# Hybrid decoder step on one core: attention's small TensorE work gathered into fewer, larger groups

## The chip, the cores and the metric

The kernel runs on one core of one Trainium2 chip. The metric is the device time in microseconds (us) of one execution; the median of three runs of the kernel before is 1492.1 us (1491.84 to 1492.78).

## What is computed

One layer of a hybrid decoder: a half-step SwiGLU network, then two branches side by side (gated linear attention, GLA, and stick-breaking attention, SB), their gated sum, and a second half-step SwiGLU network. There are 512 prompt tokens, 16 meta tokens ahead of them and 32 sample tokens (8 sequences of 4, each with 256 cached keys): 560 columns in all. The part that the change touches is the stick-breaking attention:

```python
def block(args):                                   # 16 heads of 64
    qblk, qi = args
    z = jnp.einsum('bqhd,bkhd->bhqk', qblk, k) * scale + bias_f
    mask = k_idx[None, :] < qi[:, None]
    l = jnp.where(mask, jax.nn.log_sigmoid(-z), 0.0)
    r = lax.cumsum(l, axis=3, reverse=True) - l
    a = jnp.where(mask, jnp.exp(jax.nn.log_sigmoid(z) + r), 0.0)
    return jnp.einsum('bhqk,bkhd->bqhd', a, v)
```

So a weighting is sigmoid(z) times the product of (1 - sigmoid(z)) over the later keys; the kernel gets that product from a running scan.

## The kernel before

All large products run on TensorE as three products of float32r parts (a rounded part "hi" and the rest "lo"): hi by hi, hi by lo, lo by hi. A weight tile is loaded by a DMA of the SP queue (`raw`), cast to hi on ScalarE (ACT, `S.copy`), and its lo is a subtraction on VectorE (DVE, line 172). Each group of six such matmuls ends with a `yield`, and the loop then calls `step()`. The text counts in these steps: **a step is six main matmuls**. Whatever else is to be done is put in tables of step numbers (`then(n, f)` for attention, `when(n, f)` for the mixer after it, `later(n, f)` relative to now), and a function that comes due at a step issues all its instructions there. Every engine but SP runs its instructions in exactly that program order, so the table of step numbers is the order on each queue.

The stick-breaking stage takes eight pairs of heads (`Pair`, `pr` 0 to 7). The main stream of a pair is 8 steps of query products (`queries`, lines 728 to 731) and 14 steps of key and value products (`values_keys`, `seven_steps`, lines 1079 to 1081: seven half products in place of eight, in the order a by b1, d by b1, b by t, d by b2, c by t, a by b2, c by t4, two steps each; `a`, `d`, `b`, `c` are PSUM banks, `b1`, `t`, `b2`, `t4` weight parts). While the main stream of pair `pr + 1` runs, the attention of pair `pr` is strewn in at steps `n + d`, where `n` is the first step of that stream:

- `scores(e, 0..2)` (e is the head of the pair; lines 2009 and 2010): four or two matmuls into one PSUM bank, then two sigmoids on ACT (`keep`, `beta`, lines 2013 and 2014) and masks on GpSimd (POOL, line 2018).
- `scan(e, 0..3)` (line 2027) on DVE: the running products. `weigh(e)`: one long DVE multiplication (128x1343) that gives the weightings.
- `turned(e, 0..2)` (line 2089): transposes of the weightings on TensorE, each copied out by ACT (line 2092). `meta_turned` does this for the meta tokens (lines 2115, 2116).
- `summed` (line 2105) and `meta_summed` (lines 2120, 2122): the value sums.
- `rows_v`, `rows_k`, `tails` (lines 2055, 2044, 2064 to 2066): transposes that bring values and keys to the outputs' layout.
- in pairs 4 to 7, `sample_keys` (line 2192, copied by ACT at 2194): transposes of cached key pages, and `sample_products` (line 2206): scores against them.
- `sample_rows` and `sample_rows_out` (lines 2157, 2159, 2171): once, masks for the samples.

All these small outputs share four PSUM banks (`ps`), taken in turn. `Arena` hands out SBUF places; which place a tile gets is a table of bytes, `PLACES`, written ahead of time for this order of takes.

The weight parts of the next pair are cast and subtracted in the same steps: b1 at 2 and 3, t at 5 and 6, b2 at 10 and 11, t4 at 13 and 15. The loads of half of these weights add into `raw` by a DMA of POOL (`st.add`, line 674).

Of the kernel before, what the change touches and what calls it, by code (L numbers as in the profile page):

```python
# [50 lines left out]


PLACES = bytes.fromhex("""
0c4236301f4f2a3d163453647c0256726c6088544a94901c187648867866922414128c8e748a5c00847e684106706e7a80620408244c581a5b07
2e826a28265c4e231e0a062a5e5a3e3c30401e082292784e8c66748e1284207e6886008a0c43104c62047a6e1a585c708036253a826a601c1802
549456640c6c4a9033422c852a5272302e76484e2615882f1046297c840c246c892b13363a42723b282a3038324e102e472f6c1452242b88892a
3a122d4e283332720e0c304246526d73242e114e88103b72322c3a422852316c262a254e46241110723230423a526c6d880e31254e2924517210
504442526d893a305144286c4f88722489504e3b51263a5428426c464488728e8c941e867a80744f68606457517866008a705a6e921c3a361a18
55381614123c0c641a1c2a324e3057182451550c641931241c1b565251311a552419271a55192752511c1a1d1b0c5a2a3e64001a3c1b01030400
0205552750201e384636221970788a72644e5084488e0824260a3d88606c7e3052666a3a824b45473779421f86928c901b7a3e43123923738b21  # L60
7180191d181a30577c7407683c32761233941606146e55624031807e584c30886052564a0732336d6c5552666a068c8256923e3286907a5a3010
6c2e0c54720a5e86365c2a2c0e78181a3a32462851444f201904420070718a1e221c388b299110024e54724c490a323a1a462e567a824800664b
9290296a185185420c061e847071588e443005288c6c040854028a725e2c0e2a1c4c103e4e0082931858390c866691516a90707142843849784a
92185a205c22004854362826026c8a8c58042e7237448208390c0a387a568691246a66253a901e1a78648a8e5593421c49584a348c6c82707204
32304c085e8452864e507a91923e562a0d061e37420a581a2f5530240c088c4c4a49100e5642323458372a04450749060c1e420e47442a2c551a
1c588c06560c044c242e4207371e1a49553230443435100e068c3a4238371c3004550c2432492b1e1a55078c1c2c0637100e4230463804443a34
2a4332071e090c248c55491c1a34062b303242492a0b8c0e244d303a04441e1a1c384637422c8c58100c3255062e304649372a422c3034350810
0e0b2a8c061e1a1c380444372e3a2c56240c0849432a0a3a55308c2e0437428c0624351e381a1c462c442a04434b308c49080a322e550d1e2a49
37303442042e1e30340e1009448c2c1a1c324638068c0a553a240c344b49205c571a2c463a4d3443378438087a902a495e26285c8430044b2e32
5456451a0a068c4284381e5e20364d082c5c321c587a905c2a20491a18422e8c4530324b080a4d36062c04907a04308c84385e04061e2e2c5c2a  # L70
20494237341e063008494b2c32465e5c42394d0a20364432044b3b494a2c00023708221e065c5a303244483600043b4a4c372c4302390a06485a
5e44205c1e2242000a1c263b06048d541a3656185884907a8c484c0f0e06104a243a0c8c283837392c0e04900a08020007367a062a34103b3a2f
0c46080a2a2c37062e7b2f0c4e307c827a62923994663e706e8668403c728a166a7678457e1480125c742a5a1a5e6c1c182660427f89841e4c64
75582220568e7489886c2e542c747f45483b0a02248a8926496036427e1982048c72067c892a1a181c7e805e085b5a1589785c768e886a80147e
3f5f86896987683c9412258b7d3a09734616900788830b006212287a92704266906484741e3e7e2280385654264c6c6a36201a2a184a6010944e
0c78028e521a312e500e0a048c061612143a5a7624085e44682b35832c542a728656883d34421c8a437c481830763283405d772c3d543f69575b
8a432a685a7688554230821b5f69342e8b3e198a3d3c761c182a4654595a68578b4288835f8a3c32182a3e1954821a348b444059696876305f2a
888a83823c188b421a5a6859463e5f2a76548a69403c8842828b5989461a5f545a2a402c6876888a6a828e028010060c8c922a94907866707404
427e6c120a7a22524e3a1e40285e5a5c54202e2a1c30783666221e1a3c7018192c2a22207823181f1e21792a2e1e201f78232179222a54123e20
34322242471e78703c335a64443082922062  # L80
""")


# [53 lines left out]
def hybrid_step(  # L137
# [1377 lines left out]
    with tc.manual_schedule(engines={E.PE, E.DVE, E.Activation, E.Pool}):  # L1515
# [278 lines left out]
        for j in range(5):  # L1794
            n = P if j < 4 else NTL
# [387 lines left out]
    def pages_of(src, c, b0):  # L2183
        return {(b, pg): page(src, 2 * b + pg, c) for b in (b0, b0 + 4) for pg in range(2)}
# [304 lines left out]

    z, kT = take(512), {}  # L2490
    E = mybir.EngineType
    SK, SP, TURN = (4, 7, 13, 14), (9, 16), (15, 16, 17, 18, 19, 20)

    TILE, PAIR, MIX0 = 8, 14, 24
    BEGIN = [0, 3 * TILE]
    while len(BEGIN) < 9:
        BEGIN.append(BEGIN[-1] + TILE + PAIR)
    with tc.manual_schedule(engines={E.PE, E.DVE, E.Activation, E.Pool}):
        kps, mixer_at, at = {}, {}, {}

# [100 lines left out]
        n = 0  # L2601
# [29 lines left out]
        n = 8 * len(PAGES)  # L2631
# [43 lines left out]
        n = 0  # L2675
# [126 lines left out]
```

## Time and profile before

| | |
|---|---|
| median of 3 runs | 1492.1 us |
| the profiled execution: its time, its span | 1492.38 us, 1490.7 us |
| TensorE matmuls (PE) busy | 1477.2 us, 99% of the span, 11825 matmuls |
| DVE, ACT, POOL busy | 74%, 55%, 6% |
| granted TensorE clock | 0.999 |
| stick-breaking stage | some 590 to 820 us after the start |

The profile names engines PE (matmuls), PEld (weight loads), DVE, ACT, POOL and SP. A row of the timeline has start, duration, engine, source line, operation, tiles, shape, count, and in brackets the idle time of the engine before it and what ended it. Durations of neighbouring matmuls overlap, since they are pipelined: what a matmul costs TensorE is the distance from its start to the next start.

### The profile page before, as it was taken

What the parts mean: (1) busy time and instruction counts of PE and PEld (TensorE: products, weight loads), DVE (VectorE), ACT (ScalarE), POOL (GpSimd) and SP (SyncE); (2) the same over time, 40 slices, a digit from 0 to 9 for tenths busy, and PEclk for the clock granted to TensorE, in tenths of its full rate; (3) what the DMA queues carried; (4) which work ended last, traced back from release to release, by engine and by line L of the source; (5) the groups of instructions that cost most, each with busy time, mean ns of one, the idle gap of its engine ahead of it and who ended that gap; (6) DMA issues with size and microseconds to landing.
All of it is one profiled execution on the core that took longest, in us unless ns stands there. A gap on an engine that the chain in (4) does not pass through costs nothing.

```text
span 1490.7 us, 29755 instructions
## 1 busy us (share of the span) xinstructions
PE 1477.2 (99%) x11825; PEld 1426.3 (96%) x11825; DVE 1099.8 (74%) x1844; ACT 822.7 (55%) x1537; POOL 86.6 (6%) x175
## 2 busy tenths in 40 slices
PE   9999999999999999999999999999999999999998
PEld 8999999999999899889888999999999999999998
DVE  6888888855677866888887754676567898888544
ACT  7455445533555657777777543644564455455334
POOL 2000000000000111422111000000000000000000
PEclk9999999999999999999999999999999999999999
DMA  8133333224665596557577857434531333333253
GB/s 252 44 99 96 104 88 104 85 79 128 175 141 129 159 201 141 115 109 148 139 112 187 249 136 205 96 104 137 166 109 54 100 100 100 100 105 93 80 168 100
DMA packets 288541, 187.61 MB, mean 126 GB/s; under 512 B 10988, under 2 KB 266674, under 8 KB 288402
## 3 DMA queue, kind: packets, MB, share of 16 engines
q1 hardware_dynamic: 280706, 181.97, 45.8%
q0 software_dynamic: 7680, 3.74, 2.4%
q8 instruction: 93, 1.52, 0.4%
q14 instruction: 46, 0.38, 0.1%
q10 hardware_dynamic: 16, 0.00, 0.0%
HBM read 160.63 MB, written 25.03 MB: 125 GB/s over the span
## 4 chain that ended last, share of the span: by engine, by line
PE 53%; DVE 3%; ACT 1%; DMA 1%; issue 0%; DVEq 0%; SPq 0%; ACTq 0%
PE acc L1300 4%; PE acc L1301 4%; PE acc L1302 4%; PE acc L1079 3%; PE acc L744 3%; PE acc L742 3%; PE acc L741 3%; PE acc L1080 3%; PE acc L1081 3%; PE acc L728 3%; PE acc L731 3%; PE acc L729 3%; PE ps L2105 1%; DVE room L172 1%; PE ps L2089 1%; PE acc L1239 1%
## 5 line engine op out<-in xcount | busy, mean ns | idle before, releaser
L172 DVE TENSOR_TENSOR room<-room,room 128x560 f32<-128x560 f32 (+15 forms) x469 | 303.3, 666 | 82.1 <-ACT room L808 17.8
L172 DVE TENSOR_TENSOR lo<-raw,hi 128x1024 fp32r<-128x1024 f32 (+1 forms) x207 | 248.2, 1200 | 101.3 <-ACT hi L1006 62.4
L1301 PE MATMUL acc<-room,hi 128*128 128x280 f32 (+1 forms) x896 | 259.7, 290 | 0.0
L1300 PE MATMUL acc<-room,hi 128*128 128x280 f32 (+1 forms) x896 | 259.4, 290 | 0.0
L1302 PE MATMUL acc<-room,lo 128*128 128x280 f32 (+1 forms) x896 | 259.0, 289 | 0.0
L1006 ACT CAST hi<-raw 128x1024 fp32r<-128x1024 f32 x114 | 119.5, 1052 | 141.2 <-PE acc L1301 48.4
L728 PE MATMUL acc<-room,hi 128*128 128x280 f32 x608 | 175.7, 306 | 0.3 <-DVE room L175 0.3
L1302 PEld LDWEIGHTS acc<-room,lo 128*128 128x128 f32 x896 | 168.7, 188 | 0.0
L1301 PEld LDWEIGHTS acc<-room,hi 128*128 128x128 f32 x896 | 168.5, 188 | 0.0
L1300 PEld LDWEIGHTS acc<-room,hi 128*128 128x128 f32 x896 | 168.4, 188 | 0.0
L729 PE MATMUL acc<-room,hi 128*128 128x280 f32 x608 | 163.6, 288 | 0.0
L1079 PE MATMUL acc<-room,hi 128*128 128x280 f32 x476 | 146.2, 307 | 0.4 <-ACT acc L1069 0.2
L1081 PE MATMUL acc<-room,lo 128*128 128x280 f32 (+1 forms) x476 | 138.3, 290 | 0.0
L1080 PE MATMUL acc<-room,hi 128*128 128x280 f32 (+1 forms) x476 | 138.1, 290 | 0.0
L706 ACT CAST hi<-raw 128x1024 fp32r<-128x1024 f32 (+1 forms) x93 | 93.6, 1007 | 78.3 <-issue 20.4
L1006 ACT CAST hi<-room 128x1024 fp32r<-128x1024 f32 x106 | 88.7, 836 | 82.1 <-PE acc L1301 58.7
L172 DVE TENSOR_TENSOR lo<-room,hi 128x1024 fp32r<-128x1024 f32 x106 | 101.1, 954 | 43.7 <-ACT hi L1006 43.4
L731 PE MATMUL acc<-room,lo 128*128 128x280 f32 x608 | 125.9, 288 | 0.0
L728 PEld LDWEIGHTS acc<-room,hi 128*128 128x128 f32 x608 | 114.5, 188 | 7.3 <-issue 5.6
L729 PEld LDWEIGHTS acc<-room,hi 128*128 128x128 f32 x608 | 114.8, 189 | 0.6
L741 PE MATMUL acc<-room,hi 128*128 128x280 f32 (+2 forms) x388 | 110.8, 295 | 0.1
L742 PE MATMUL acc<-room,hi 128*128 128x280 f32 (+2 forms) x388 | 108.8, 290 | 0.0
(409 smaller groups left out, 3606.8 us busy)
## 6 DMA issues: line engine op xcount, KB each, us to landing
raw<-in_w_in_dram SPq DMA_DIRECT2D x68, 256.0 KB, 5.0
raw<-in_ffn_w_gate_dram SPq DMA_DIRECT2D x64, 256.0 KB, 3.1
raw<-in_ffn_w_up_dram SPq DMA_DIRECT2D x64, 256.0 KB, 3.4
raw<-in_ffn_w_down_dram SPq DMA_DIRECT2D x36, 448.0 KB, 3.7
raw<-in_w_in_dram SPq DMA_DIRECT2D x29, 512.0 KB, 6.9
out_dram<-room SPq DMA_DIRECT2D x36, 256.0 KB, 3.4
room<-in_cache_k_dram SPq DMA_DIRECT2D x32, 256.0 KB, 6.7
room<-in_cache_v_dram SPq DMA_DIRECT2D x32, 256.0 KB, 6.1
```

The source lines that it names most:

```text
L172: (eng or V).tensor_tensor(out=out, in0=a, in1=b, op=op)
L728: T.matmul(acc[h][:, :w], hi[k], act.get(k, h, w)[0], start=(k == order[0]), stop=False, skip_group_check=True)
L729: T.matmul(acc[h][:, : wid[h]], hi[k], a[h][1], start=False, stop=False, skip_group_check=True)
L731: T.matmul(acc[h][:, : wid[h]], lo[k], a[h][0], start=False, stop=(k == order[-1]), skip_group_check=True)
L741: T.matmul(acc[h][:nw, : wid[h]], wh, a[h][0], start=(k == 0), stop=False)
L1006: S.copy(hi[:, :kt], src)
L1079: T.matmul(x[:, :n], hi, act_[k][0][:, :n], start=(first and k == 0), stop=False, skip_group_check=True)
L1080: T.matmul(x[:, :w], hi, act_[k][1][:, :w], start=False, stop=False, skip_group_check=True)
L1081: T.matmul(x[:, :w], lo, act_[k][0][:, :w], start=False, stop=(k == 3), skip_group_check=True)
L1300: T.matmul(x[:, :QW], hi, act[k][0], start=(first and k == 0), stop=False, skip_group_check=True)
L1301: T.matmul(x[:, :QW], hi, act[k][1], start=False, stop=False, skip_group_check=True)
L1302: T.matmul(x[:, :QW], lo, act[k][0], start=False, stop=(k == 3), skip_group_check=True)
```

## The change

New numbers in the tables of steps. The scores, the transposes and the sums of a pair come due at fewer steps, so that TensorE meets them in fewer, larger groups between main matmuls (steps 3, 6, 11, 16, 19 for pairs 0 to 3, and 14 besides in pairs 4 to 7). DVE's scans and `weigh` keep the last steps that they had (14 and 15), with some earlier ones moved. `sample_keys` in the mixer and `sample_rows_out` move by one step. `PLACES` is written anew for the new order. No instruction is added or taken out.

```diff
-    SK, SP, TURN = (4, 7, 13, 14), (9, 16), (15, 16, 17, 18, 19, 20)
+    SK, SP, TURN = (14, 14, 14, 14), (16, 16), (16, 16, 16, 19, 19, 19)
...
-            now, n, after = Pair(pr), BEGIN[pr + 1], BEGIN[pr + 2] if pr < 7 else BEGIN[8] + 20
+            now, n, after = Pair(pr), BEGIN[pr + 1], BEGIN[pr + 2] if pr < 7 else BEGIN[8] + 18
...
-            pieces = [(2, now.scores, 0, 0), (3, now.scores, 0, 1), (3, now.meta), (4, now.scan, 0, 0), (4, now.scan, 0, 1), (5, now.scores, 0, 2),
-                      (6, now.scan, 0, 2), (7, now.scan, 0, 3), (6, now.rows_v), (7, now.scores, 1, 0), (9, now.scan, 1, 0), (10, now.scan, 1, 1),
-                      (10, now.weigh, 0), (10, now.scores, 1, 1), (12, now.scan, 1, 2), (11, now.rows_k), (12, now.scores, 1, 2), (12, now.tails),
-                      (14, now.scan, 1, 3), (15, now.weigh, 1)]
+            pieces = [(3, now.scores, 0, 0), (3, now.scores, 0, 1), (4, now.meta), (5, now.scan, 0, 0), (5, now.scan, 0, 1),
+                      (6, now.scores, 0, 2), (6, now.scores, 1, 0), (6, now.rows_v), (8, now.scan, 0, 2), (8, now.scan, 0, 3), (9, now.scan, 1, 0),
+                      (10, now.weigh, 0), (11, now.scores, 1, 1), (11, now.scores, 1, 2), (11, now.rows_k), (11, now.tails),
+                      (13, now.scan, 1, 1), (13, now.scan, 1, 2), (14, now.scan, 1, 3), (15, now.weigh, 1)]
             pieces += [(TURN[i], now.turned, i // 3, i % 3) for i in range(6)] + [(TURN[5], now.meta_turned)]
...
-            then(after + 1, now.summed)
-            then(after + 2, now.meta_summed)
+            then(after + 3, now.summed)
+            then(after + 3, now.meta_summed)
...
                 for d, (q, b) in zip(SK, ((q, b) for q in range(2) for b in (pr - 4, pr))):
                     then(n + d, sample_keys, b, q, kps, kT)
                 for q in range(2):
                     then(n + SP[q], sample_products, 0, pr - 4, q, kT, z)
...
-        then(BEGIN[2] + 13, sample_rows_out)
+        then(BEGIN[2] + 14, sample_rows_out)
...
-                for n, k in enumerate((1, 2, 5, 6)):
+                for n, k in enumerate((2, 2, 5, 5)):
                     when(8 * i + k, use_keys, b0, n)
...
 PLACES = bytes.fromhex("""
-0c4236301f4f2a3d163453647c0256726c6088544a94901c187648867866922414128c8e748a5c00847e684106706e7a80620408244c581a5b07
+1e1218555a06420c505e52908e8070488a7a7e667668946a3264868c4c7c6038842a883462283c742672240a544e6e000292042c4a6c78823e2c
```

How this moves instructions is seen at three places. On TensorE, in the stream of a pair, the transposes of the first head's weightings (line 2089, `ps<-ident,room`) stand between main matmuls of `seven_steps`. Before:

```order
L2089 MATMUL ps_6918<-ident,room_72_4268 128x128 x4
L1079 MATMUL acc_6811<-room_121_6658,hi_6840 128x280
L1080 MATMUL acc_6811<-room_122_6659,hi_6840 128x280
L1081 MATMUL acc_6811<-room_121_6658,lo_6841 128x280
L1079 MATMUL acc_6811<-room_124_6689,hi_6840 128x280
L1080 MATMUL acc_6811<-room_83_4730,hi_6840 128x280
L1081 MATMUL acc_6811<-room_124_6689,lo_6841 128x280
L2089 MATMUL ps_6934<-ident,room_72_4268 128x128 x3
```

On TensorE, at the same place of the change:

```order
L1081 MATMUL acc_6809<-room_121_6659,lo_6830 128x280
L2089 MATMUL ps_6925<-ident,room_5_73 128x128 x4
L2089 MATMUL ps_6931<-ident,room_5_73 128x128 x3
L2089 MATMUL ps_6936<-ident,room_5_73 128x128 x3
L1079 MATMUL acc_6811<-room_110_6520,hi_6760 128x280
L1080 MATMUL acc_6811<-room_111_6521,hi_6760 128x280
```

Ten transposes that stood in three groups with a step between them now stand in one; those of the second head likewise, one step later than their first stood before.

On ACT, at the start of a pair's stream, stand the copy of the value sums (line 2122), the sigmoids of the first scores (2013, 2014) and the casts to hi of two weight parts (1006: b1 from `raw`, t from a room). Before:

```order
L2122 COPY room_127_7496<-ps_7720 128x512
L2013 ACTIVATE room_129_7738<-ps_7739,sbb 128x416
L2014 ACTIVATE room_79_4590<-ps_7739,sbb 128x416
L1006 CAST hi_7748<-raw_7431 128x1024
L2013 ACTIVATE room_129_7738<-ps_7757,sbb 128x416
L2014 ACTIVATE room_79_4590<-ps_7757,sbb 128x416
```

On ACT, at the same place of the change:

```order
L1006 CAST hi_7727<-raw_7429 128x1024
L2122 COPY room_76_4272<-ps_7736 128x512
L2013 ACTIVATE room_125_7283<-ps_7747,sbb 128x416
L2014 ACTIVATE room_5_73<-ps_7747,sbb 128x416
L2013 ACTIVATE room_125_7283<-ps_7756,sbb 128x416
L2014 ACTIVATE room_5_73<-ps_7756,sbb 128x416
L1006 CAST hi_7786<-room_127_7567 128x1024
```

The cast of b1 moved ahead of the copy of the sums and of all sigmoids; the cast of t now stands behind four sigmoids at a stretch.

On ACT in the middle of the stream (step 10 to 12) stand the first copy between banks (1069), the cast of b2, the last two sigmoid pairs, the copy of the key rows (2046) and the copy of bank `d` (1059). Before:

```order
L1069 COPY acc_7838<-acc_7836 128x280
L2013 ACTIVATE room_81_4592<-ps_7870,sbb 128x416
L2014 ACTIVATE room_58_3146<-ps_7870,sbb 128x416
L1006 CAST hi_7878<-raw_7550 128x1024
L2046 COPY room_99_5486<-ps_7891 128x512
L1059 COPY room_81_4592<-acc_7837 128x280
L2013 ACTIVATE room_81_4592<-ps_7911,sbb 128x512
L2014 ACTIVATE room_58_3146<-ps_7911,sbb 128x512
```

On ACT, at the same place of the change:

```order
L1069 COPY acc_7837<-acc_7835 128x280
L1006 CAST hi_7868<-raw_7564 128x1024
L2013 ACTIVATE room_124_7055<-ps_7881,sbb 128x416
L2014 ACTIVATE room_81_4592<-ps_7881,sbb 128x416
L2013 ACTIVATE room_124_7055<-ps_7889,sbb 128x512
L2014 ACTIVATE room_81_4592<-ps_7889,sbb 128x512
L2046 COPY room_127_7567<-ps_7895 128x512
L1059 COPY room_9_92<-acc_7836 128x280
```

The copy of bank `d`, which stood ahead of the last two sigmoids, now stands behind them and behind the copy of the key rows.

More of the change, by code (lines that the diff above doesn't have):

```diff
@@ L58 @@
[L58 to L72, printed above, removed]
@@ new lines @@
+32683c8e1e1880408a5a701003254e64277e86360e1a050428761b3e8a1f3a2318535c1c64360265700019260c0d4e1b017176283b5a64180038
+3924231e0270190c1a36770d4e1876535b04013822715a5d641f1e0c1a707718100219384e712176645c1e0c5a702353100077183971763b6421
+1e0c4e705323105a380c1a717776183a64651e23703818534e100e0c7684946c90788e6458468274167c7a4c500a88183c123008684a8c442c48
+2e9270747a242a361e2c004c5a5d4823502e2036424b222a1e214b4d222a4c202d50511e4b5150224d1f201e212400301e50181c224b38373b36
+393a19181b82667468603c5c14123e160690625a42501c442e4618887a84802d1b7e76947857153f6961673d928c0a72221e08200d4a13758317
@@ new lines @@
+49704c484b4d5d548e865c8a6e566a0e2d6c0c2c7c401910645570801a2a18847a54585c57562d888978795494725856768c0a2c187e9220221e
+0428887824269046003234304e743a6862186053146612023b364a4c3f3e0848162c8209395c1e9238787e2a5a3626765618424c3c245d685428
+4a60538c48666394881a14623f3e3a72501c22291e045d926078384a30342a2c7e58680a234e905c486654823a8c08282409636294885b551674
+4604480032222047535a3e601e7802382e4a50665d429236194e3a5c764c9063088c82091c625e5672943c745b182e3846025406287e78926636
+262458304c4a6888901676631214343a5b4e2b193802302a4e460a08573644555854423a3430061902265b2b425534522438503b262a060a5430
@@ new lines @@
+1b364e3a02192450570844425b2b19364e3402525618080a4630242e26292a2c4250380654025b1942242e34572938521a1c2c36024e30502a06
+0a2d5b5d083418582c2a42245b072e38245256291c1806342a503a02542608240a4e3028504345341a3628065b2b4e420a303a0656072c2a3738
+241c1934265402283a0845365c305e432e1a24454e37075b30585642062a2c1843191b4536383a5434025e5c1d4f565158282e0a0618424e5b08
+0230024345560642262434580a36545c5e3a381c34360a1a58062e2c3a184f515e06323058011a54004a4c5c185e5a76622a28604a44423a3856
+3e4e460234081c62560a60763663064a4c32625c525036185a5e320002463a441d08364a38421c4c345c0604621c080676604c56440a185c3a5a
@@ new lines @@
+1c0832065e424438585c08301a360a3a4c1c4656544b1a3208344a5d5c3022061e5848204a4442385c3a340b1a460a44080642304c1c32480a1e
+203a54585632481a4a2c34634476602a246150280a26020462060801004460522200762e30634c1c02184e3e5a604246621a4a4c635e004d0405
+18026260364b44764a4d395a18006e64108a1612687c787e6a740c7a408e8c88707284576726941e926d3406083266800a2c4a37829150140e4c
+668648206c54828356242a28903a36573c8c60623e3d662d82804a37670822762c6e8e64661e339226670635949532080b8872706655847a0774
+54610c0d41403f7e68426f0a778d658f46588a0706080b16124f747c3830548a104c3a780e423648866c267a142a9084822e5a1a24804a7e7288
@@ new lines @@
+683462662c2001187092527658604e5450563e466e0c7a5b8e1d65641a1e1c8c320822245a4243065f7a943d0402203c46181c26648f451e0008
+225c1a03441f4006233c0a8f478e2028642400422202441c433c40235a03041a64245d0b5c0a461e5f42008f8e653e5a3d20040b64400226245c
+4625416544428f3c0a8e40210222645c0425652400448f3c208e47400a0241465c5d5e24648e668874606c386834842e7e8a042c901800200e76
+3c827c5430620a48725c0846108636784e5e06042818261e015c245a064600035c25282700245a05290403260424030025292826274206544e04
+40033e241d28041a3c002c52137a8c18261c
```

12 lines of the change are left out of this document (1 added, 11 removed).

## The prediction, made before the changed kernel was run

> **What bounds the kernel now.** I read the page first, then the busy time of the stage in question, the table of waits of TensorE in it, and then the timeline of one pair, engine by engine. First the page's line of TensorE, and the stage from 590 to 870 us (columns: stretch, length, busy us with counts for PE, PEld, DVE, ACT and POOL, clock, DMA share, GB/s):
>
> ```profile
> PE 1477.2 (99%) x11825; PEld 1426.3 (96%) x11825; DVE 1099.8 (74%) x1844; ACT 822.7 (55%) x1537; POOL 86.6 (6%) x175
> ...
> 590.00:870.00 280.00, 275.97 (x2307) 252.08 (x2307) 227.03 (x405) 203.56 (x386) 56.27 (x94) 1.00 0.67 149
> ```
>
> TensorE is the bound at full clock. So only two things can change the time: what an instruction costs TensorE, and the waits that are left on it. In the stage it stands idle for 4.0 of 280 us by busy time. Who it waits for there (total us, times, longest):
>
> ```profile
> PE ps L2089 <- DVE room L172: 2.3, 4, 0.8
> PE ps L2171 <- POOL room L2159: 0.9, 1, 0.9
> PE ps L2206 <- ACT room L2194: 0.6, 2, 0.3
> ```
>
> These three are the work that the change moves: the turned weightings, the sample masks, the products with cached keys. Ends of matmuls are modelled, so I size each loss from start to start.
>
> **Part 1: does a group cost less than its pieces?** TensorE in the third pair (`pr` 2), scores and transposes among main matmuls:
>
> ```profile
> 655.03 0.39 PE L2009 MATMUL ps<-room 128*128 128x512 f32 x1
> 655.26 0.39 PE L2010 MATMUL ps<-room,room 128*128 128x512 f32 x1
> ...
> 658.85 0.29 PE L1080 MATMUL acc<-room,hi 128*128 128x280 f32 x1
> ...
> 659.37 0.29 PE L1081 MATMUL acc<-room,lo 128*128 128x280 f32 x1
> ```
>
> From 658.85 to 659.37 four main matmuls start, 0.13 each, so a step of six is 0.77. Scores cost 0.23 for 512 columns (655.03 to 655.26). Then the transposes:
>
> ```profile
> 659.50 0.49 PE L2089 MATMUL ps<-ident,room 128*128 128x128 f32 x3
> ...
> 659.96 0.29 PE L1080 MATMUL acc<-room,hi 128*128 128x280 f32 x1
> ...
> 661.59 0.29 PE L1081 MATMUL acc<-room,lo 128*128 128x280 f32 x1
> 662.63 0.65 PE L2089 MATMUL ps<-ident,room 128*128 128x128 f32 x4 [0.76 <-DVE room L172]
> ...
> 663.26 0.29 PE L1080 MATMUL acc<-room,hi 128*128 128x280 f32 x1
> ...
> 664.87 0.29 PE L1081 MATMUL acc<-room,lo 128*128 128x280 f32 x1
> 665.00 0.49 PE L2089 MATMUL ps<-ident,room 128*128 128x128 f32 x3
> 665.33 0.60 PE L2115 MATMUL ps<-ident,room 128*96 128x128 f32 x4
> ...
> 665.89 0.29 PE L1080 MATMUL acc<-room,hi 128*128 128x280 f32 x1
> ```
>
> Three transposes: from the main matmul before (659.37) to the second one after (659.96) 0.59, less two normal distances of 0.13, is 0.33, or 0.11 each. Seven in one group: 664.87 to 665.89 is 1.02, less 0.26, is 0.76, or 0.11 each. The first main matmul after a group does hold up its successor by 0.08, which looks like a price of the change of work; but it is the last transpose's share, since it doesn't appear once more per group. So merging transposes is worth 0 (bounds: 0.01 a group either way, some 1 us in all). The Trainium skill ("TensorE: Matmul & The Clock Gate", section on LDWEIGHTS) puts a load of 128 stationary columns at 128/1.2, some 107 ns, whatever stands beside it; by that rule each transpose pays its own load in any group and the sum here is 0 as well, where a reader of the 0.08 would book a gain, and the trace's 0.11 agrees with it.
>
> The products with cached keys are another form (32 columns wide):
>
> ```profile
> 707.68 0.29 PE L1081 MATMUL acc<-room,lo 128*128 128x280 f32 x1
> ...
> 709.39 0.40 PE L1079 MATMUL acc<-room,hi 128*128 128x280 f32 x1
> ...
> 738.39 0.29 PE L1081 MATMUL acc<-room,lo 128*128 128x280 f32 x1
> ...
> 739.61 0.40 PE L1079 MATMUL acc<-room,hi 128*128 128x280 f32 x1
> ...
> 768.58 0.29 PE L1081 MATMUL acc<-room,lo 128*128 128x280 f32 x1
> ...
> 770.27 0.40 PE L1079 MATMUL acc<-room,hi 128*128 128x280 f32 x1
> ...
> 799.15 0.40 PE L731 MATMUL acc<-room,lo 128*128 128x280 f32 x2
> 799.48 0.40 PE L2206 MATMUL ps<-room 128*32 128x256 f32 x1
> ...
> 799.72 0.38 PE L2206 MATMUL ps<-room 128*32 128x256 f32 x1
> ...
> 800.05 0.40 PE L728 MATMUL acc<-room,hi 128*128 128x280 f32 x1
> ```
>
> The last group runs unhindered: from the second main matmul before (799.28) to the one after (800.05) 0.77, with 0.24 for each four. So 0.29 is beside the eight, paid on going in and out. The change puts both groups of eight of a pair into one, in four pairs: at most 4 x 0.29 = 1.2, at least 0. I take half, **-0.6**.
>
> **Part 2: the waits that the change takes away.**
>
> *Products (L2206).* The same distance is 1.71, 1.22 and 1.69 in pairs 4, 5 and 6, against 0.77: 0.94 + 0.45 + 0.92 = 2.3 lost, waiting for ACT's copy of the turned keys (L2194). In the change all sixteen key transposes stand at step 14, and the products at step 16 behind two steps (1.54) and ten transposes (1.1), so ACT's four copies have 2.6 us more. **-2.3** (bounds: 0 to -2.3).
>
> *Turned weightings (L2089).* The stalled group of pair 2: 661.59 to 663.26 is 1.67, less 0.26, less four transposes 0.44, is 0.97 lost for a row that shows 0.76. The 2.3 us of the table, four times in pairs 0 to 3, are so 2.3 x 0.97/0.76 = 2.9. The wait is for `weigh(1)`, the long multiplication on DVE. DVE in this pair:
>
> ```profile
> 643.09 0.69 DVE L172 TENSOR_TENSOR room<-raw,raw 128x512 f32<-128x512 f32 x1
> 646.83 1.23 DVE L172 TENSOR_TENSOR lo<-raw,hi 128x1024 fp32r<-128x1024 f32 x1 [3.04 <-ACT hi L1006]
> 647.97 1.16 DVE L2027 TENSOR_TENSOR_SCAN room<-room,room 128x144 f32<-128x144 f32 x2
> ...
> 656.37 1.23 DVE L172 TENSOR_TENSOR lo<-raw,hi 128x1024 fp32r<-128x1024 f32 x1
> ...
> 658.62 0.28 DVE L2070 COPY room<-ps 48x128 f32<-48x128 f32 x1
> ...
> 661.02 1.56 DVE L172 TENSOR_TENSOR room<-room,room 128x1343 f32<-128x1343 f32 x1
> ```
>
> and ACT, which made it wait 3.04 us at the start:
>
> ```profile
> 644.15 0.58 ACT L2122 COPY room<-ps 128x512 f32<-128x512 f32 x1 [3.19 <-PE ps L2120]
> ...
> 645.75 1.05 ACT L1006 CAST hi<-raw 128x1024 fp32r<-128x1024 f32 x1
> ...
> 652.70 0.38 ACT L1069 COPY acc<-acc 128x280 f32<-128x280 f32 x1 [0.49 <-PE acc L1081]
> ...
> 655.54 0.41 ACT L1059 COPY room<-acc 128x280 f32<-128x280 f32 x1
> ...
> 656.41 0.71 ACT L2014 ACTIVATE room<-ps,sbb 128x512 f32<-128x512 f32 x1
> ```
>
> ACT stands idle 3.19 us for the value sums, with the cast of b1 queued behind their copy and two sigmoids; DVE waits for that cast, and from 646.83 it has no idle time until `weigh(1)` ends at 662.58. The change puts the cast ahead of the copy, into ACT's idle time, so DVE goes on at 643.8. It then meets waits of its own. The sums and first scores stand a step later, so ACT's chain starts at 644.15 + 0.77 = 644.9; copy and one sigmoid take 1.2, first scan at 646.1; DVE gets there after its lo (1.2) and some 0.7 of a sum and copies, at 645.7: 0.4 idle. The scans (1.1) end at 647.2, but the cast of t now stands behind four sigmoids: copy and two sigmoids took 1.6 (644.15 to 645.75), two more 1.0, the cast 1.05, so 648.6: 1.4 idle. The tails' copies wait for TensorE's group at step 11: some 0.4. Together 2.2, so DVE is 3.04 - 2.2 = 0.8 earlier at `weigh(1)`, 661.8. TensorE asks for it at step 19, not 18: 661.72 + 0.77 = 662.5. So 0.97 late becomes 0.7 in hand. **-2.9** (bounds: 0 to -2.9).
>
> *Sample masks (L2171).* 0.9 once, in pair 1. The step that asks is one later (0.77) and behind scores (1,1) and (1,2), issued at 11 and no later than before; POOL's work ahead of it is the same. **-0.9** (bounds: 0.9 comes back, or not). The Trainium skill ("SBUF — State Buffer", section on two separate sides) has DVE and GpSimd share a port pair by an exclusive lock; by it POOL could be held again wherever DVE runs without a break, the 0.9 would stay, and the sum be 0.9 smaller. One row speaks for something of the kind, a mask of 32x64 that takes long:
>
> ```profile
> 624.50 2.77 POOL L2157 TENSOR_SCALAR_AFFINE_SELECT room<-room 32x64 f32<-32x64 f32 x1
> ```
>
> **Part 3: the waits that it may add.** Three places get tight in pairs 0 to 3.
> - lo of b2 (DVE) now stands behind the tails' four copies. From the end of TensorE's group at step 11 to the matmul that reads it: three steps and two matmuls, 2.6. DVE: four copies at 0.28 or less, 1.1 with the subtraction among them, and 1.23: 2.3. In hand 0.3.
> - ACT's copy of bank `d` (1059), which TensorE must await before it adds b2 to `d` at step 14, now ends the lump after L1069: the same seven instructions took from 652.70 to 656.41 + 0.6, 4.3. TensorE has four steps (3.1), seven transposes (0.77) and scores of 1856 columns, 0.23 for 512, so 0.83: 4.7. In hand 0.4. In pairs 4 to 7 sixteen transposes (1.8) come between.
> - `weigh(1)` itself, as above.
>
> I take 0.2 a pair for the three, four pairs, **+0.8** (bounds: 0, and the 2.9 of today back). The four `ps` banks suffice: no group takes more than four, and ACT's copies have two or more steps before the next. `PLACES` shifts waits on SBUF places all over the kernel; outside the stage TensorE's order is the same, and I book 0, bounds -1 and +1.
>
> **Sum:** -0.6 - 2.3 - 2.9 - 0.9 + 0.8 = -5.9. The profiled execution took 1492.38 us, 1490.7 of it the span; 0.28 above the median. Taken off the median: **1486.2 us**.
>
> **Rivals.**
> 1. *Waits move on.* DVE is busy 81% of the stage and more in pairs 0 to 3; if the three tight places eat the 2.9 and the masks' 0.9 stays, -0.6 - 2.3 = -2.9 less a little is left: 1489.5. For it: 0.3 to 0.7 in hand are no more than the estimates are worth.
> 2. *A group really saves a boundary.* If the 0.08 after each group were a price per group, some eight fewer a pair, 64 in all, would give 5 us more: 1481. Against it: 0.33 for three, 0.76 for seven.
> 3. *The lump on ACT turns it round (slower).* ACT serves in order, and its 4.3 us after step 10 stand against TensorE's 4.7 in pairs 0 to 3, and in pairs 4 to 7 the key transposes at step 14 take all four banks that these sigmoids must free. If ACT comes x late, all eight pairs lose x less what is in hand (0.4): above 1.1 late the 5.9 are gone, at 1.6 the kernel is 4 slower, 1496. Against it: ACT was idle 0.49 just before L1069 and is busy 73% of the stage.
>
> **How the numbers follow.** Forecast 0.72, rival 1 0.16, rival 2 0.05, rival 3 0.07. A measurement of this kernel can tell about 0.2%, 3 us, from no change: 1489.1 divides. Of the forecast's own cases (terms at their bounds) a twelfth lies above that, 0.06, and of rival 1 most: faster 0.66 + 0.05 + 0.06 = 0.77, same 0.16, slower 0.07. Range: all losses gone and the products merged in full give 1484.8, with the room table's 1 us 1483.8; the upper end takes in rival 1, 1490.2.
>
> **What would show it.** Right: no wait of L2089 on DVE nor of L2206 on ACT in TensorE's table; ACT's cast of b1 ahead of the copy 2122, in idle time, and DVE's idle before lo of b1 gone; ten transposes in one group costing 1.1; idle DVE time ahead of the scans and of lo of t. Wrong: new rows for L1079 waiting on ACT 1059 or on DVE's lo at step 14, or L2192 waiting for banks; or groups that cost less than their pieces.

## The result, and the profile after

The changed kernel takes 1482.2 us (median of 4 runs, 1481.83 to 1483.2), the kernel before 1492.4 beside it: ratio 0.9933, 95% interval 0.9916 to 0.995, 10.2 us less. A second measurement in five rounds gave 1481.99 us, ratio 0.9929 (0.9915 to 0.9942). The forecast was 1486.2, the range 1483.8 to 1490.2: the direction was right, the gain nearly twice as large as forecast. The profiled execution took 1483.2 us, the slowest of its four; its span is 1481.5, against 1490.7.

TensorE's line of the page and the stage after (columns as in the prediction; the stage ends some 9 us earlier):

```profile
PE 1472.6 (99%) x11825; PEld 1426.8 (96%) x11825; DVE 1097.5 (74%) x1844; ACT 818.8 (55%) x1537; POOL 86.6 (6%) x175
...
590.00:861.00 271.00, 270.00 (x2297) 250.53 (x2296) 222.89 (x401) 198.25 (x383) 55.74 (x93) 1.00 0.70 155
```

TensorE is now without work for 1.0 of 271 us; before, 4.0 of 280. The table of TensorE's waits in the stage has a single row. Before, it had the three rows that the prediction shows and this one, at 0.2, in the mixer:

```profile
PE acc L1079 <- ACT acc L1069: 1.0, 1, 1.0
```

The third pair on TensorE, around what was the stalled group of four transposes:

```profile
653.98 0.29 PE L1080 MATMUL acc<-room,hi 128*128 128x280 f32 x1
654.11 0.34 PE L1081 MATMUL acc<-room,lo 128*128 128x280 f32 x1
654.28 0.29 PE L1079 MATMUL acc<-room,hi 128*128 128x280 f32 x1
...
658.73 0.29 PE L1081 MATMUL acc<-room,lo 128*128 128x280 f32 x1
658.86 1.25 PE L2089 MATMUL ps<-ident,room 128*128 128x128 f32 x10
```

and on DVE in the same pair:

```profile
642.56 1.07 DVE L2027 TENSOR_TENSOR_SCAN room<-room,room 128x144 f32<-128x144 f32 x2 [0.91 <-ACT room L2013]
644.99 1.23 DVE L172 TENSOR_TENSOR lo<-room,hi 128x1024 fp32r<-128x1024 f32 x1 [1.36 <-ACT hi L1006]
...
651.74 0.28 DVE L2070 COPY room<-ps 48x128 f32<-48x128 f32 x1 [0.74 <-PE ps L2066]
...
652.77 1.23 DVE L172 TENSOR_TENSOR lo<-raw,hi 128x1024 fp32r<-128x1024 f32 x1
653.91 2.84 DVE L2027 TENSOR_TENSOR_SCAN room<-room,room 128x272 f32<-128x272 f32 x3
656.86 1.56 DVE L172 TENSOR_TENSOR room<-room,room 128x1343 f32<-128x1343 f32 x1
```

The 3.04 us that DVE stood idle before lo of b1 are gone. In their place are 0.91, 1.36 and 0.74 at the three places that the prediction named (0.4, 1.4, 0.4). `weigh(1)` ends at 658.42, and TensorE asks for it at 658.86: 0.44 in hand. Lo of b2 ends at 654.00, and its first reader starts at 654.11: 0.1 in hand. ACT's copy of bank `d` ends at 653.48, and the step that adds b2 to `d` starts at 653.85: 0.37 in hand. ACT's cast of b1 stands in its idle time, ahead of the copy 2122 (the third row is the copy of bank `d`):

```profile
637.44 1.05 ACT L1006 CAST hi<-raw 128x1024 fp32r<-128x1024 f32 x1
641.43 0.59 ACT L2122 COPY room<-ps 128x512 f32<-128x512 f32 x1 [2.94 <-PE ps L2120]
...
653.04 0.44 ACT L1059 COPY room<-acc 128x280 f32<-128x280 f32 x1
```

A pair with cached keys: the sixteen key transposes, and the ten weightings with the sixteen products:

```profile
739.65 0.29 PE L1081 MATMUL acc<-room,lo 128*128 128x280 f32 x1
739.78 1.25 PE L2089 MATMUL ps<-ident,room 128*128 128x128 f32 x10
740.96 1.07 PE L2206 MATMUL ps<-room,room 128*32 128x256 f32 x16
741.96 0.40 PE L1079 MATMUL acc<-room,hi 128*128 128x280 f32 x1
742.20 0.29 PE L1080 MATMUL acc<-room,hi 128*128 128x280 f32 x1
```

From 739.65 to 742.20 are 2.55; less two normal distances 2.29; less ten transposes at 0.11, the sixteen products cost 1.19. Two groups of eight would cost 0.76 each by the same reckoning, 1.52: a merge saves 0.33.

**Where the 9 us come from.** The 9924 main matmuls come in the same order in every kernel here, so the start of each can be compared with its start in the kernel before. Differences in us, negative is earlier; the columns are stretches by the times of the kernel before, and each number is what that stretch adds. They count from a main matmul at 100 us, since what lies ahead of it differs between executions of one kernel (by 0.4 us between the two profiles of the kernel before). The names are those of the experiments below.

| kernel (first profile) | 100 to 382 us | pairs 0 to 3 (585 to 694) | pairs 4 to 7 (694 to 815) | whole stage (585 to 878) |
|---|---|---|---|---|
| changed | -1.2 | -4.2 | -3.7 | -7.7 |
| changed, again | -1.2 | -4.2 | -3.7 | -7.8 |
| new order, old places | +0.2 | -4.5 | -3.8 | -8.1 |
| products alone | +0.2 | 0.0 | -0.9 | -0.9 |
| all but products | +0.6 | -4.4 | +0.2 | -4.2 |
| turned alone, first / again | -0.3 / +0.3 | -0.7 / -2.2 | +0.1 / +0.2 | -0.5 / -1.9 |
| masks and mixer | +0.3 | -0.1 | 0.0 | -0.1 |
| cast ahead alone, first / again | 0.0 / +0.1 | +0.8 / +0.8 | 0.0 / 0.0 | +0.8 / +0.8 |
| products and tails | 0.0 | +1.5 | -3.4 | -1.8 |
| before, again | -0.2 | 0.0 | 0.0 | 0.0 |

Where moved groups stand across the border of a pair, the split between pairs is good to some 0.3; the whole stage is not touched by that. Three of the rows hold, in pair 1, a spell of slow matmuls at half the granted clock (last section), which isn't in the profile of the kernel before: turned alone, first (1.4), products and tails (1.2), and both of cast ahead alone (1.2). Without it they would read -2.1, +0.3 and -0.4 in pairs 0 to 3.

### The profile page after: what moved, and what is told of

It reads as the page before. It is cut to its first block, busy times and chain, and to the rows that moved or that the text cites. A ratio compares the mean times of both kernels' runs of the same rounds, so it can differ in the third digit from the quotient of the medians.

```text
span 1481.5 us, 29805 instructions
## 1 busy us (share of the span) xinstructions
PE 1472.6 (99%) x11825; PEld 1426.8 (96%) x11825; DVE 1097.5 (74%) x1844; ACT 818.8 (55%) x1537; POOL 86.6 (6%) x175
## 3 DMA queue, kind: packets, MB, share of 16 engines
q8 instruction: 93, 1.52, 0.4%
## 4 chain that ended last, share of the span: by engine, by line
PE 95%; DVE 2%; ACT 1%; DMA 1%; issue 0%; DVEq 0%; SPq 0%; ACTq 0%
PE acc L1302 8%; PE acc L1301 8%; PE acc L1300 8%; PE acc L741 7%; PE acc L744 6%; PE acc L742 6%; PE acc L728 5%; PE acc L729 5%; PE acc L731 5%; PE acc L1079 4%; PE acc L1081 4%; PE acc L1080 4%; PE acc L1242 2%; PE acc L1239 2%; PE acc L1240 2%; PE ps L2105 1%
## 5 line engine op out<-in xcount | busy, mean ns | idle before, releaser
L172 DVE TENSOR_TENSOR room<-room,room 128x560 fp32r<-128x560 f32 (+14 forms) x464 | 300.9, 667 | 85.2 <-ACT room L1059 17.7
L728 PE MATMUL acc<-room,hi 128*128 128x280 f32 x608 | 173.1, 301 | 0.3 <-DVE room L175 0.3
L729 PE MATMUL acc<-room,hi 128*128 128x280 f32 x608 | 163.5, 288 | 0.0
L1079 PE MATMUL acc<-room,hi 128*128 128x280 f32 x476 | 141.7, 298 | 1.1 <-ACT acc L1069 1.0
L706 ACT CAST hi<-raw 128x1024 fp32r<-128x1024 f32 (+1 forms) x93 | 93.6, 1007 | 77.6 <-issue 20.4
L731 PE MATMUL acc<-room,lo 128*128 128x280 f32 x608 | 125.7, 288 | 0.0
```

Of the source, the lines that this page charges most:

```text
L172: (eng or V).tensor_tensor(out=out, in0=a, in1=b, op=op)
L728: T.matmul(acc[h][:, :w], hi[k], act.get(k, h, w)[0], start=(k == order[0]), stop=False, skip_group_check=True)
L729: T.matmul(acc[h][:, : wid[h]], hi[k], a[h][1], start=False, stop=False, skip_group_check=True)
L731: T.matmul(acc[h][:, : wid[h]], lo[k], a[h][0], start=False, stop=(k == order[-1]), skip_group_check=True)
L1079: T.matmul(x[:, :n], hi, act_[k][0][:, :n], start=(first and k == 0), stop=False, skip_group_check=True)
```

## Experiments

**The changed kernel again, and its order with the old places.** Edit of the second: `PLACES` alone, 1475 of 1526 bytes are the old ones.

> The changed kernel once more, unaltered. Of the 9.2 us between the two profiled executions some 7.5 lie in the stage (590 to 870 us) and 1.5 to 2 before it, most of that one wait of 0.73 us of TensorE at 376 us that the changed kernel's profile lacks. If the part before the stage is the work of the room table (the places in SBUF), the wait at 376 us is missing again and the kernel is 9 to 10 us faster; if it is chance, it may be there and the profiled time is nearer 1484.5.

> The new order of work with the old places in SBUF: of 1526 places 1475 are those of the kernel before, 51 in the stage had to move. If the order alone carries the gain (theory of the waits: -3.1 transposes, -0.95 masks, -2.3 and -1.3 products, -0.5 mixer, together -8.1), TensorE's timetable up to 587 us is that of before, with the wait at 376 us, and the stage is 7 to 8 us shorter: about -8, 1484. If the room table is worth 1.5 to 2 by itself, that much is missing against the changed kernel. If the room table carried the stage's gain too (a wait on a place, not on the work), the stage keeps some of its old waits and the gain is below 6.

1481.99 us (0.9929, 0.9915 to 0.9942) and 1483.69 (0.9941, 0.9927 to 0.9954), 1.7 apart on the same chip. The order alone carries 8.1 in the stage; the table of places carries the 1.2 to 1.3 before it. The wait at 376 us is there with the old places (0.74) and missing with the new.

**What in the table of places.** SP and ACT in the kernel before, ahead of that wait (the weights `in_ffn_w_down` of the first network, cast at L706):

```profile
364.15 0.37 SPq L679 DMA_DIRECT2D room<-in_w_in_dram  x1
...
366.33 0.37 SPq L205 DMA_DIRECT2D raw<-in_ffn_w_down_dram  x1
...
373.89 1.05 ACT L706 CAST hi<-raw 128x1024 fp32r<-128x1024 f32 x1 [4.42 <-DMA raw<-in_ffn_w_down_dram]
...
376.25 0.40 PE L744 MATMUL acc<-room,lo 128*128 128x280 f32 x1 [0.73 <-DVE lo L172]
```

An early load of 512 KB for a later stage (L679) goes out ahead of the weights that TensorE needs next. In the changed kernel the place of that load comes free later, and it goes out behind four of those loads, at 373.77. One run moved it and four small rooms, another put it back in the changed kernel:

```diff
 # kernel before, PLACES: the room of fetch_early (L679)
-62
+26      # and four small rooms that stood there
```

> The changed kernel with the place of one early load (512 KB of w_in, L679) put back to that of the kernel before; 63 of 1526 places change, the order of work on the four compute engines doesn't. In the changed kernel this load is issued at 373.8 us, behind four loads of the down projection's weights; in the kernel before at 364.1, ahead of them, and the weights come 2.9 us later. Here it stands behind the first of them. If that one transfer is what the room table's 1.3 us hangs on, most of the wait at 376 us is back: +0.6 to +1.3 against the changed kernel, 1482.6 to 1483.3, all of it before 382 us. If it is something else in the table, the time of the changed kernel.

> The kernel before with one early load of w_in (512 KB, L679) in another place in SBUF, one whose last holder comes free later; four small rooms had to make way, 1521 of 1526 places and the order of the compute engines stay. The load is then issued behind four loads of the down projection's weights, as in the changed kernel, and not ahead of them. If the 1.3 us that the room table is worth hang on this transfer, ACT's cast of those weights comes at 371, not 373.9, the wait of TensorE at 376 us is gone, and the kernel is 1.0 to 1.5 us faster than before: about 1491.1. If they hang on something else in the table, no change and the wait is there.

The run on the kernel before (load later): 1490.51 us, 0.9987 (0.9978 to 0.9996), 2.0 less. Main matmuls are 1.35 earlier by 382 us, and the wait is gone:

```profile
365.69 0.38 SPq L205 DMA_DIRECT2D raw<-in_ffn_w_down_dram  x1
...
373.20 0.58 SPq L679 DMA_DIRECT2D room<-in_w_in_dram  x1
...
370.45 1.05 ACT L706 CAST hi<-raw 128x1024 fp32r<-128x1024 f32 x1 [1.63 <-DMA raw<-in_ffn_w_down_dram]
```

Five bytes of the table give what the whole new table gives. The run with the place put back (63 places of the changed kernel moved; its values for the samples come out wrong, so only its timetable up to 382 us is read) missed: 1483.37 us, where most of the wait at 376 us was expected, and it stayed away. Its load went out at 367.05, still behind the first weight load (366.62), whose cast came at 371.40; 0.8 us were lost earlier, where other rooms had moved. So what seems to count is to be behind that first load.

**Products alone, all but the products, and the products with the tails.**

```diff
 # products alone (kernel before)
-    SK, SP, TURN = (4, 7, 13, 14), (9, 16), (15, 16, 17, 18, 19, 20)
+    SK, SP, TURN = (14, 14, 14, 14), (16, 16), (15, 16, 17, 18, 19, 20)
...
-                for n, k in enumerate((1, 2, 5, 6)):
+                for n, k in enumerate((2, 2, 5, 5)):
 # products and tails: this, and
-                      ... (12, now.scores, 1, 2), (12, now.tails),
+                      ... (11, now.scores, 1, 2), (11, now.tails),
 # all but products (changed kernel)
-    SK, SP, TURN = (14, 14, 14, 14), (16, 16), (16, 16, 16, 19, 19, 19)
+    SK, SP, TURN = (4, 7, 13, 14), (9, 16), (16, 16, 16, 19, 19, 19)
```

> The kernel before with the products with cached keys alone moved (key transposes to step 14, products in one group at step 16; the same in the mixer's steps); turned weightings, masks and scores stay. 30 places had to move. Waits: -2.3 for the three waits on ACT's copies, -1.3 for four merges at 0.33, -0.5 in the mixer: -4.1, about 1488.2; the waits for weigh(1) and for the masks stay as they are. My prediction's terms: -2.9. A price of 0.08 for each group and nothing else for the merge: -2.3 - 0.5 - 20 x 0.08 = -4.4.

> The changed kernel with the products and key transposes put back where they were before (4, 7, 13, 14 and 9, 16; mixer's 1, 2, 5, 6); places nearly those of before, 41 moved. Theory of the waits: -3.1 for the waits on weigh(1) and -0.95 for the masks, nothing for the merging of scores and transposes: -4.0, about 1488.3, and the waits of the products on ACT stay (2.3 by distances). My prediction's terms: -2.9 - 0.9 + 0.8 = -3.0. A price of 0.08 for each group: 8 pairs x 8 groups x 0.08 = 5 more, -9.

> The run with the products alone gained 0.9 in the stage instead of 3.6 (-2.3 and -1.3), since its sixteen key transposes took 2.66 to 2.71 in three pairs, against 1.75 in the changed kernel: they need all four banks, one of which DVE still reads for the tails. Here the tails and the last scores stand one step earlier (11, not 12), as in the changed kernel; else as that run, 30 places moved. If the bank is the cause, the three losses of 0.9 shrink by 0.77 each: another -2.3 or so against that run, about 1488.8; if DVE is just as late with the tails, no more than -0.5.

Products alone: 1491.35 us, 0.9993 (0.9984 to 1.0003), unclear, and 0.9 in the stage where 3.6 were expected. The waits on ACT are gone and the merges are paid out, but a new wait stands at the key transposes, in three pairs:

```profile
PE ps L2192 <- DVE room L172: 2.1, 3, 0.7
...
742.90 1.47 PE L2192 MATMUL ps<-ident,room 128*128 128x128 f32 x12
745.11 0.66 PE L2192 MATMUL ps<-ident,room 128*128 128x128 f32 x4 [0.73 <-DVE room L172]
```

Sixteen transposes need all four banks, and DVE still subtracts from one of them for the tails. The group takes 2.66 to 2.71 there, 1.75 in the changed kernel. With the tails one step earlier (1489.44 us, 0.9976, 0.9967 to 0.9985) it takes 1.75, and pairs 4 to 7 gain 3.4, nearly all of what the whole change gains there (3.7). But in pairs 0 to 3 the waits for `weigh(1)` are then replaced, not removed (3.0 by distances, for 3.1):

```profile
PE acc L1081 <- DVE lo L172: 2.5, 3, 0.9
```

This is the first of the prediction's tight places, lo of b2 behind the tails' copies: without the cast of b1 ahead, DVE is late there. All but the products: 1487.91 us, 0.9969 (0.9957 to 0.9981): pairs 0 to 3 gain 4.4, and pairs 4 to 7 nothing, since the transposes of their tails now wait for banks (`L2064 <- ACT L2014`, 1.2 by its rows). Pairs 0 to 3 of this run and pairs 4 to 7 of the one before make up the whole: -4.4 - 3.4 = -7.8.

**Turned weightings alone, the cast ahead alone, the cast put behind again.**

```diff
 # turned alone (kernel before)
-    SK, SP, TURN = (4, 7, 13, 14), (9, 16), (15, 16, 17, 18, 19, 20)
+    SK, SP, TURN = (4, 7, 13, 14), (9, 16), (16, 16, 16, 19, 19, 19)
 # cast ahead alone (kernel before; cast behind is the reverse, in the changed kernel)
-            pieces = [(2, now.scores, 0, 0), ...
+            pieces = [(3, now.scores, 0, 0), ...
-            then(after + 1, now.summed)
-            then(after + 2, now.meta_summed)
+            then(after + 3, now.summed)
+            then(after + 3, now.meta_summed)
```

> The kernel before with nothing but the turned weightings regrouped (16 and 19 in place of 15 to 20); the same places. TensorE asks for weigh(1) one step (0.77) later, while DVE's timetable stays, with its idle time before lo of b1. The four losses of 0.79, 0.35, 0.97 and 0.99 by distances would shrink to 0.02, 0, 0.2 and 0.22: -2.7, about 1489.7; if the cast of b1 had to go ahead for the wait to vanish, little is gained: 0 to -0.5.

> The kernel with nothing but the turned weightings regrouped, once more. Its first profile shows 2.6 less in the groups of pairs 0 to 3, but 15 main matmuls behind the sample masks' wait at 0.23 instead of 0.13 each, at a granted clock of 0.52, which gave 1.6 back. If that spell is chance, it is not there now (or elsewhere) and the pairs gain 2.6; if this order brings it about, it is there again.

> The kernel before with the first scores one step later and the value sums at step 3, so that ACT's cast of b1 stands ahead of the sums' copy; turned weightings, masks and products stay at their old steps, the same places. If the cast is what makes DVE late, DVE's 3 us of idle time before lo of b1 shrink, weigh(1) is 1 us or more earlier and its four waits go: -3.1, about 1489.4. If DVE only waits elsewhere (for the sigmoids, for the cast of t), the waits stay and the time too. From the run with the cast put behind in the new order (+3.3 against the changed kernel) the first is likelier.

> The changed kernel with the value sums back at steps 1 and 2 and the first scores at 2, so that ACT's cast of b1 stands behind the sums' copy and two sigmoids again; all else as changed, the same places. If putting the cast ahead is what made DVE early, DVE again idles some 3 us before lo of b1, weigh(1) ends later than in the changed kernel, by 0.5 to 1 us, and since TensorE asks for it at step 19, waits of 0 to 0.3 come back in each of pairs 0 to 3: 0 to +1. If it matters nothing, the same time as the changed kernel within 0.3 and no wait on weigh(1).

Turned alone: 1491.19 us, 0.9986 (0.9977 to 0.9996). The waits for `weigh(1)` shrink to some 0.2 in two pairs, and 0.25 to 0.35 come back before the value sums in three (L731); by its second profile the four pairs gain 2.2 (expected 2.7). The cast behind, in the changed kernel: 1485.41 us, 0.9951 (0.9936 to 0.9965), 2.9 above the scattered run beside it, and a stage 3.2 longer than the changed kernel's, where 0 to 1 was expected. The wait that comes back isn't the one I had named, `weigh(1)`, but lo of b2 again, four times:

```profile
PE acc L1081 <- DVE lo L172: 2.3, 4, 0.7
...
655.86 0.40 PE L1081 MATMUL acc<-room,lo 128*128 128x280 f32 x1 [0.74 <-DVE lo L172]
```

By distances the four are 0.76, 0.43, 0.90 and 0.83, together 2.9. So in the new order the cast ahead, with the sums and first scores that move with it, is worth 2.9 to 3.2 of the 4.2 in pairs 0 to 3. In the old order the same move gains nothing: the cast ahead alone took 1493.26 us, 1.0005 (0.9996 to 1.0014), where I expected 3.1 less. The three waits for `weigh(1)` in pairs 0, 2 and 3 shrank by only 0.4 each (the three pairs gain 0.4, 0.6 and 0.6 in all), since DVE waits for ACT at its new places (1.07 and 1.39 in pair 1). In pair 1 the masks' wait grew by 1.2, and the slow matmuls behind it cost 1.2 more:

```profile
PE ps L2171 <- POOL room L2159: 2.1, 1, 2.1
```

**Masks and mixer alone** (kernel before, `sample_rows_out` at 14, `use_keys` at 2, 2, 5, 5).

> The kernel before with two small edits far apart, the same places: the sample masks one step later (14 in place of 13, once, in pair 1), and the key transposes of the mixer's products at steps 2, 2, 5, 5 in place of 1, 2, 5, 6. Masks: the group (some 1.2 when unhindered, 2.19 now) loses 0.77 to 0.95 if POOL is done in time, and nothing if POOL, held by DVE, is just as late. Mixer: the group at 847 us takes 2.74, of which 0.5 to 0.67 is a wait for ACT's copy and goes. Together -1.3 to -1.6, about 1490.9; if POOL stays late, -0.5.

1492.2 us, 0.9994 (0.9984 to 1.0003): nothing. The masks' group falls from 2.19 to 1.43, so the next group of weightings falls due sooner, DVE's `weigh(1)` doesn't, and that group's cost rises from 0.79 to 1.38. In the mixer the wait on a key copy goes (2.74 to 2.07) and 0.7 comes back 2 us later, as it does in the changed kernel:

```profile
837.83 1.07 PE L2206 MATMUL ps<-room,room 128*32 128x256 f32 x16
...
841.75 0.40 PE L1079 MATMUL acc<-room,hi 128*128 128x280 f32 x1 [1.00 <-ACT acc L1069]
```

**The price of a boundary, and of a merge.**

```diff
 # turned scattered (changed kernel)
-    SK, SP, TURN = (14, 14, 14, 14), (16, 16), (16, 16, 16, 19, 19, 19)
+    SK, SP, TURN = (14, 14, 14, 14), (16, 16), (16, 17, 18, 19, 20, 21)
 # products split (changed kernel): SP = (16, 17)
```

> The changed kernel with its two groups of turned weightings (steps 16 and 19) scattered to six (16, 17, 18, 19, 20, 21), each later than in the changed kernel and so without a wait; the same places. It prices the boundary of a group by itself: 8 pairs x 4 more groups = 32 boundaries. If a boundary costs nothing (transposes 0.11 each in any group), no change: 0, at most 0.3. If it costs 0.08, +2.6. If the copies of the late groups come too late for the value sums, a wait for ACT shows at the sums (L2120).

> The changed kernel with the sixteen products of a pair with cached keys split again into two groups of eight (steps 16 and 17), both without a wait since the second only stands later; the same places. If a group of this form pays on going in and out once per group (16 products 1.19 in the changed kernel, 8 products 0.76), four pairs cost 4 x 0.33 = +1.3: 1483.3 to 1483.5. If half of it, as I predicted, +0.6; if nothing, 0, and the gain of pairs 4 to 7 has another source.

Scattered: 1482.54 us, 0.993 (0.9916 to 0.9944), and 7.8 in the stage like the changed kernel: 32 boundaries more cost nothing. Products split: 1483.58 us, 0.9939 (0.9925 to 0.9953); the stage is 1.26 longer than in the changed kernel, 0.32 for each of four pairs, with no new wait. So the merge of products is worth its full price, and the merge of transposes none (ten in one group take 1.10, as in three: 0.44 + 0.33 + 0.33).

**The kernel before again, and the cast ahead again**, for single profiles.

> The kernel before, a second profile. If the old places cause the wait of some 0.7 us at 376 us it is there again, as in the four kernels with old places run since; the stage shows the same waits as in the first profile, 2.3 for L2089, 0.9 for L2171, 0.6 for L2206, and spells of a lower clock behind them if such a wait can bring them.

> The kernel with the cast put ahead alone, once more, for the spell of a lower clock. Its first profile shows a wait of TensorE of 2.1 us for the sample masks and right behind it some 2.5 us of matmuls at 0.22 to 0.23 instead of 0.13 (granted clock about half). If a wait of that length brings the spell, it is there again; if it was chance, matmuls run at 0.13 behind the same wait.

Both repeat: before again has the same four waits (2.3, 0.9, 0.6 and 0.2 us) and the late cast at 373.30; the cast ahead again has the wait of 2.07 for the masks and behind it the spell of slow matmuls (below).

## Why the prediction was wrong, and where it was right

- *Products, waits (-2.3)*: -2.3. The three waits are gone, group by group (0.93 + 0.43 + 0.91).
- *Products, merged (-0.6)*: **mis-sized**, -1.3. The prediction worked out 0.29 per merge from an unhindered group and then took half; the group of sixteen gives 0.33, the split run 0.32. The half had no row behind it.
- *Turned weightings (-2.9)*: -3.1 by distances (0.79 + 0.35 + 0.97 + 0.99). Size and steps hold: the cast of b1 in ACT's idle time, DVE earlier, TensorE asking a step later. The weights of the steps don't: asking later does nearly all of it by itself (0.2 left in two pairs, 2.2 gained), the cast ahead alone takes 0.4 off each wait, and what the cast is worth in the new order (2.9 to 3.2) lies at lo of b2, which would be late without it.
- *Masks (-0.9)*: -0.95. POOL still has a slow row (two masks in 3.17 us, where the median of this form is 0.43 each), but ahead of the sample masks now:

```profile
619.85 3.17 POOL L2018 TENSOR_SCALAR_AFFINE_SELECT room<-room 128x128 f32<-128x128 f32 x2 [0.33 <-ACT room L2014]
...
623.32 0.40 POOL L2157 TENSOR_SCALAR_AFFINE_SELECT room<-room 32x64 f32<-32x64 f32 x1
```

DVE ran scans and the 1343-column product (621.35 to 622.87) beside the slow row, which ended just behind it at 623.0; in the kernel before, that product (625.48 to 627.00) lay beside the mask that took 2.77. The lock between DVE and GpSimd that the Trainium skill states ("SBUF — State Buffer", section on two separate sides) agrees with both rows. That the lock is what slows these rows is not shown by a run of its own. The prediction made of it that the 0.9 might stay; the slow rows move with DVE's timetable: away from the masks here, onto them in the run with the cast ahead alone (wait 2.1).
- *New tight places (+0.8)*: **mis-sized**, 0. All three held, one by 0.1 us. The sizes "in hand" (0.3, 0.4, 0.7) were about right (0.1, 0.37 and 0.44 in the third pair); to charge 0.2 a pair for places that come out in hand was caution put into the sum.
- *Not booked*: the mixer's wait at 847 us, 0.67, goes and comes back as 0.77: nothing, by luck.
- *Room table (0, bounds -1 and +1)*: **mis-sized**, -1.3 by the profiles, 1.7 by the times. This is the step that failed in kind and not only in size: the sentence "outside the stage TensorE's order is the same" was true of TensorE and not looked up for SP's queue, where the early load stands ahead of the weights in one table and behind four of their loads in the other.

Together -2.3 - 1.3 - 3.1 - 0.95 - 1.3 = -9.0 for the -5.9 of the forecast; the changed kernel's first profile is 8.9 earlier at its last main matmul, its second 9.9 (0.7 of the difference is one wait for DVE at 1443 us, which the first has and the second doesn't). The medians differ by 10.2, so some 1.2 have no cause here. The range failed at its low end by 1.6 us: it took every loss as gone (1484.8), and only 1 us for the rooms. With -9.0 taken off the same 1492.1 the time would be 1483.1: the terms account for 0.7 of these 1.6 us, and the rest stays open.

The rivals: *waits move on* was wrong for the whole change, and right for nearly every part of it done alone (four parts done alone gain 2.1 in the stage, -0.9 - 1.9 - 0.1 + 0.8, or 3.3 without the slow spell in the last; together 7.7). *A group saves a boundary* would have given 1481, near the measured time, for a reason that the scattered run excludes. *ACT's lump* didn't come late in the changed kernel; the bank waits of the run without the products show how near pairs 4 to 7 are to it.

## What to carry to other kernels

A wait is a place where lateness comes out, not where it is made: one part of a reordering often only sends it to the next consumer, so book the set of moves and test it as a set. If an order or an allocation is generated anew, compare the DMA queue's order over the whole program too; one early load of 512 KB in front of the weights needed next cost 1.3 us far from the edit. Matmul groups of one form (128-column transposes) gain nothing from being merged, groups of another form (32 columns wide) pay 0.3 us once for each group.

## What the hardware showed that I had not expected

A wait of 0.9 us and nine tiny matmuls behind it can halve TensorE's clock for 3.4 us. In the run with the turned weightings alone, main matmuls behind the masks' wait (0.89) started 0.23 apart, not 0.13, and the granted clock was 0.52; in the second profile of the same kernel, behind the same wait, it was 1.00:

```profile
628.70:632.20 3.50, 3.50 (x17) 3.49 (x17) 3.37 (x9) 0.69 (x2) 3.50 (x4) 0.52 0.47 115
...
629.15:632.15 3.00, 3.00 (x25) 2.98 (x25) 2.87 (x9) 0.69 (x2) 3.00 (x4) 1.00 0.39 90
```

Seven profiles here have this wait of 0.9; three of them have the spell behind it (turned alone, products and tails, load later; +1.2 to +1.4 us), four don't. Behind the wait of 2.07 it came in both. Ahead of the spell stand not only the wait but 1.0 us of nine matmuls of 32x32 and 1x1: none of the 41 other waits of 0.65 to 1.07 us in these profiles has a spell behind it, nor have the nine matmuls without a wait. What decides is on record, too. In all 18 profiles the granted clock changes only at whole multiples of 3.413 us from its first rise, and each spell lasts one such window (3.41). Where 1.95 us or more of the wait and the tiny matmuls fall into one window, the next runs at half clock (five of five); where they are cut by a window's end and at most 1.80 fall into one, it doesn't (four of four). The Trainium skill ("TensorE: Matmul & The Clock Gate", Part 1) has the clock fall to half after an idle window of some 3.4 us and rise again after as much; the length of the spell agrees, the idle time that brings it is shorter here. The changed kernel has no wait at the masks and no spell in the stage. So some runs of the kernel before must be expected to have the spell, though neither of its profiles does; that this is part of the 1.2 us without a cause is likely and not shown.
